# Retention's queries and keys: out of the visited groups, into four wide groups behind them; the gates in their places

## The chip, the cores and the metric

One Trainium2 chip, one of its cores. The metric is the time of one execution on the device in microseconds (us), as the median of several runs. The core's engines are TensorE (PE in the profile, with its weight loads as PEld), VectorE (DVE), ScalarE (ACT), GpSimd (POOL) and SyncE (SP, whose queue issues the loads).

## The reference

One decoder layer for a batch of 1 and 256 tokens, d_model 2048, all in float32, then a final RMSNorm:

```
mod = silu(c) W_ada + b_ada          -> shift1, scale1, gate1, shift2, scale2, gate2
h   = RMSNorm(x)(1+scale1)+shift1
p   = h W_in      # [retention q,k,v,g | HGRN2 q,f,i,g | branch gate A | branch gate B]
yA  = W_retO( LN_head(Retention(rope(q),rope(k),v)) * silu(g) )      # 4 heads of 256
yB  = W_hgO( RMS_head(HGRN2(silu(q), f, i)) * silu(g) )              # 8 heads of 128
x   = x + gate1 * ( (sigmoid(gA)*yA + sigmoid(gB)*yB) W_out )
h2  = RMSNorm(x)(1+scale2)+shift2
[a, b] = split(causal_depthwise_conv3(h2 W_up))                      # d_ff 5632
out = RMSNorm_final( x + gate2 * ((silu(a) * b) W_down) )
```

Retention and HGRN2 run in chunks of 128 tokens. This case is about `p = h W_in`, whose first eight parts are 1024 columns wide each and whose two branch gates are 2048.

## The kernel before

**Numbers and tiles.** Each float32 product is made of three float32r products. Weights and activations are both split into an upper part (the value rounded to float32r) and a lower part (the remainder): upper x upper, upper x lower and lower x upper are added in PSUM. Weights come in pieces of two K tiles (2 x 128 rows) by 512 columns, 512 KB each. `pieces` loads a piece into `raw` (12 buffers), ACT copies it to `wh` (upper part, line 167, 4 buffers) and DVE subtracts to `wl` (lower part, line 172, 4 buffers). An activation tile `hT` has for each K tile 512 columns: 256 tokens of upper parts, then 256 tokens of lower parts. A group is 512 columns of weights over all 16 K tiles.

**Two forms of matmul.** `mm_rows` (lines 196 to 198) makes token rows: the activations (128 tokens) are the stationary operand and 512 weight columns stream; six matmuls of 512 columns a K tile. `mm_cols` (lines 209 to 211) makes channel columns, the transpose: the weights (128 columns) are stationary and 256 tokens stream; twelve matmuls of 256 columns a K tile. The up projection has a third form (lines 1081 and 1083): weights stationary, upper and lower activations side by side stream as one matmul of 512 columns, and the lower weights with the upper activations as one of 256. The two halves of the 512 stand apart in PSUM and are added afterwards.

**PSUM.** `pg` is a tile of two banks with two buffers, `po` one of one bank with four. `mm_rows` and `mm_cols` need one `pg` for a group; the small matmuls of HGRN and retention use `po`.

**Order of the work.** The modulation vectors (`ada1`, DVE dot products of loaded rows, line 421) make the activations one K tile after another, about one in 15 us. So the first twelve groups, `ATT`, are *visited*: the loop goes round them, takes in each as many K tiles as there are by then, and adds the partial product to the group's SBUF tile `p` (`take`: at first an ACT copy, line 789, afterwards a DVE add, line 791). The twelve are HGRN's f, q, i and retention's q, k, v, two groups of 512 columns each; i and v are in rows (`ROWS`), the other eight in columns. When all of a block's three groups are complete, its generator is started: `hgrn` or `retention`, for two halves `hb` of the heads. The last visits, with all 16 K tiles there, go through the groups in order and take from one to five K tiles each.

Behind the loop come four gate groups (`wb`, rows; ACT applies Silu from PSUM to `gt`, line 878), eight branch gate groups (`wab`, rows; Sigmoid, line 892), the output projections of both branches, `wout`, the up projection and the down projection.

The generators in `back[0]` (HGRN, retention, their gating) and `back[1]` (the dot products of gate1 and ada2) are traced in slices by `pump`, which is called once a piece of weights; queue 0 works through one generator after the other. All of it runs on the engines beside the groups' matmuls. `hgrn` uses its gate in its last step (line 682), `gated` that of retention (line 745). Instructions not pinned are ordered by a scheduler at compile time; at run time each engine's queue is in order.

Of the kernel before, what the change touches and what calls it, by code (L numbers as in the profile page):

```python
# [16 lines left out]
AF = mybir.ActivationFunctionType  # L17
ALU = mybir.AluOpType

P = 128  # L20
D = 2048
T = 256
NT = T // P
KT = D // P
# [5 lines left out]
G = 512  # L30
# [8 lines left out]

C_RQ, C_RK, C_RV, C_RG, C_HQ, C_HF, C_HI, C_HG = (i * W1 for i in range(8))  # L40
C_GA, C_GB = 8 * W1, 8 * W1 + D
ATT = (C_HF, C_HF + G, C_HQ, C_HQ + G, C_HI, C_HI + G, C_RQ, C_RQ + G, C_RK, C_RK + G, C_RV, C_RV + G)
ROWS = (C_HI, C_HI + G, C_RV, C_RV + G)
GW = 2 * G
LEVELS = (64, 32, 16, 8, 4, 2, 1)
TWO_PI = 2.0 * math.pi
# [9 lines left out]
class Kernel:  # L56
# [143 lines left out]
    def mm_cols(self, ps, act, wh, wl, first, last):  # L200

        nc = self.nc
        hi, lo = act[:, :T], act[:, T:]
        for j in range(4):
            cs = slice(j * P, (j + 1) * P)

            opens = first and j % 2 == 0
            out = ps[j // 2][:, j % 2 * T : (j % 2 + 1) * T]
            nc.tensor.matmul(out, lhsT=wh[:, cs], rhs=hi, start=opens, stop=False, skip_group_check=True)  # L209
            nc.tensor.matmul(out, lhsT=wh[:, cs], rhs=lo, start=False, stop=False, skip_group_check=True)  # L210
            nc.tensor.matmul(out, lhsT=wl[:, cs], rhs=hi, start=False, stop=last, skip_group_check=True)  # L211

    def products(self, mm, ps, src, act, k0, kts, hold=0, first=True, last=True, gain=None):

# [306 lines left out]
    def hgrn(self, hb, hf, hq, v, gates):  # L521

        nc = self.nc
# [2 lines left out]
        k = self.blk([P, 4, T], name="k")  # L526
        b = self.blk([P, 4, T], name="b")
        nc.scalar.activation(f, hf, AF.Sigmoid)
        yield 3.0
        for h in range(4):  # L530
            g = slice(4 * hb + h, 4 * hb + h + 1)
# [16 lines left out]
        f = None  # L548
        q = self.blk([P, 4, T], name="q")
        nc.scalar.activation(q, hq, AF.Silu)  # L550
        yield 2.0
        at = self.blk([P, 4, T], name="at")
        nc.gpsimd.memset(at, 0.0)
# [9 lines left out]
        ps = self.po()  # L563
# [5 lines left out]
        ps = self.po()  # L569
# [4 lines left out]
        for c in range(2):  # L574
            dst = at[:, :, c * P : (c + 1) * P].rearrange("p h (z x) -> p h z x", x=32)
            msk = self.ident.bitcast(I32).rearrange("p (z x) -> p z x", x=32)[:, None].to_broadcast([P, 4, 4, 32])
            src = ps[:, 4 * c * 32 : 4 * (c + 1) * 32].rearrange("p (h x) -> p h x", h=4)[:, :, None, :].to_broadcast([P, 4, 4, 32])
# [3 lines left out]
        kt = self.blk([P, 4, T], name="kt")  # L581
        nc.gpsimd.memset(kt, 0.0)
        for lev, n in enumerate(LEVELS[:-2]):
# [15 lines left out]
            ps = self.po()  # L599
            for h in range(4):  # L600
                for c in range(2):
                    j = 2 * h + c
# [11 lines left out]
            if n >= 32:  # L614
                for z in range(0, P, 2 * n):
                    for c in range(2):
                        dst = at[z : z + n, :, c * P + z + n : c * P + z + 2 * n]
                        src = ps[z + c * n : z + (c + 1) * n, : 4 * n]
# [28 lines left out]
        ps = self.po()  # L647
        for z in range(2):
            for j in range(4 * z, 4 * z + 4):
                h, c = j // 2, j % 2  # L650
                for x in range(0, P, 32):
# [3 lines left out]
                        lhsT=kt[:, h, c * P + x : c * P + x + 32],  # L655
                        rhs=eq[:, j, :].rearrange("p (l x) -> p l x", l=2)[:, :, x // 2 : x // 2 + 16],
                        start=True,
                        stop=True,
# [3 lines left out]
            self.masked(at, len(LEVELS) - 2 + i, n, ps[:, : 8 * 32].rearrange("p (j l x) -> p j l x", j=8, l=2)[:, :, i, :])  # L662
            yield 0.9
        yield 2.8
        while len(gates) <= hb:
            yield None
        o = self.blk([P, NT, G], name="oh")
        for t in range(NT):
            ps = self.po()
# [85 lines left out]
    def run(self):  # L755
        nc, a = self.nc, self.a
# [23 lines left out]

        accs = [self.blk([P, NT, G] if c0 in ROWS else [P, 4, T], name="p") for c0 in ATT]
        done = [0] * len(ATT)
        mms = [self.mm_rows if c0 in ROWS else self.mm_cols for c0 in ATT]

        def take(g, ps, fresh):
            for at, z in self.parts(ps, ATT[g] in ROWS):
                dst = accs[g][:, at, :]
                if fresh:
                    nc.scalar.activation(dst, z, AF.Copy)  # L789
                else:  # L790
                    nc.vector.tensor_tensor(dst, dst, z, ALU.add)
# [7 lines left out]
        ps = [self.po2(), self.po2(), self.pg(), self.pg()][:FIRST]  # L799
        for k in range(2):  # L800
# [12 lines left out]
            for g in range(FIRST):  # L813
                if g >= ahead:
                    rests.append(self.rest(uppers[g] if g < len(uppers) else self.upper(a["wa"][g][:, k : k + 1, :], 1, G)))
                wh, wl = rests[g]
# [14 lines left out]

        work = 2 * FIRST
        g = FIRST
        att, gates = [], []
        small = False
        while min(done) < KT:
            if work > SMALL and not small:
                small = True
                self.small_loads(nc.sync, ("freq", "lbT", "lmask"))
                self.start(self.trig())  # L840
                self.start(self.lower_bound())
            have = min(KT, 2 + int((work - LAG) / ADA_EVERY))
            m = have - done[g]
            if m > 0:
                self.finish(*ada[:have])
                if g < RESIDENT:
                    self.products(mms[g], ps[g], a["wa"][g], act, done[g], m, first=False, last=have == KT)
                    if have == KT:
                        take(g, ps[g], True)
                else:  # L850
                    take(g, self.products(mms[g], self.pg(), a["wa"][g], act, done[g], m), done[g] == 0)
                done[g] = have
                work += m
                for hb in range(2):
                    for kind, first in ((self.hgrn, 0), (self.retention, 6)):
                        gs = [first + hb, first + 2 + hb, first + 4 + hb]
                        if g in gs and min(done[i] for i in gs) == KT:
                            self.pace(0, 14.0, 24)
                            att.append(self.start(kind(hb, *(accs[i] for i in gs), gates)))
            else:  # L860
                work += 0.5
            g = (g + 1) % len(ATT)
            if have == KT and done[0] < KT:
                g = min(i for i in range(len(ATT)) if done[i] < KT)
        self.xT = None
        del accs
        self.small_loads(nc.sync, ("gn2", "convw"))

# [2 lines left out]
        self.pace(0, 143.0, 88)  # L871
        self.pace(1, 68.0, 96)
        sgb, sga = [], []
        for j in range(4):
            ps = self.rows(a["wb"][j], act)
            gt = self.blk([P, NT, G], name="gt")
            for at, z in ps:
                nc.scalar.activation(gt[:, at, :], z, AF.Silu)
            gates.append(gt)

        og = [[], []]

# [6 lines left out]
        for j in range(8):  # L889
            gt = self.blk([P, NT, G], name="gt")  # L890
# [40 lines left out]
        for j in range(4):  # L931
            last = j == 3
            x1.append(self.load_rows(j))
            if not last:
                g = self.row(self.gate["gate1"], j, "g1")
            if j == 2:
                g3 = self.row(self.gate["gate1"], 3, "g1")
            elif last:
                g = g3
            ps = self.products(self.mm_rows, self.po2() if last else self.pg(), a["wout"][j], actm, 0, KT, hold=4 * last, gain=g if last else None)  # L940
            if last:
                g = None
# [229 lines left out]
def _groups(w, starts):  # L1172
    return np.stack([_pack(w[:, s : s + G]) for s in starts])
# [23 lines left out]
def _arrays(x, c, positions, w_ada, b_ada, g_norm1, w_in, w_ret_o, w_hg_o, w_out, hg_lb, g_norm2, w_up, conv_w, conv_b, w_down, g_final):  # L1197
    cols = lambda v: np.ascontiguousarray(v.reshape(-1, P).T)
    wada, win, wup = w_ada[0], w_in[0], w_up[0]
    out = {  # L1200
        "xT": _pack(np.ascontiguousarray(x[0].T)),
        "c": c.reshape(1, D),
        "pos": positions.reshape(1, T),
        "gn1": cols(g_norm1[0]),
        "gn2": cols(g_norm2[0]),
        "lbT": np.ascontiguousarray(hg_lb.reshape(2, HH, P).transpose(2, 0, 1)),
        "convw": np.ascontiguousarray(np.concatenate([conv_w[0], conv_b], axis=0).reshape(4, 2 * FT, P).transpose(2, 0, 1)),
        "gf": g_final.reshape(1, D),
        "xR": np.ascontiguousarray(x[0].reshape(NT, P, D).transpose(1, 0, 2)),
        "wb": _groups(win, [C_HG, C_HG + G, C_RG, C_RG + G]),  # L1210
        "wab": _groups(win, [z + j * G for z in (C_GB, C_GA) for j in range(4)]),
        "whg": _groups(w_hg_o[0], [j * G for j in range(4)]),
        "wret": _groups(w_ret_o[0], [j * G for j in range(4)]),
        "wout": _groups(w_out[0], [j * G for j in range(4)]),
        "wdown": _groups(w_down[0], [j * G for j in range(4)]),
        "wup": np.stack([_pack(np.concatenate([wup[:, 2 * i * P : 2 * (i + 1) * P], wup[:, FF + 2 * i * P : FF + 2 * (i + 1) * P]], axis=1)) for i in range(FT // 2)]),
    }
    out["wa"] = _groups(win, ATT)
    adaT = np.concatenate([wada.T, b_ada[0][:, None]], axis=1).reshape(6, KT, P, D + 1)
    out["ada1"] = np.ascontiguousarray(adaT[[1, 0]].transpose(1, 0, 2, 3))  # L1220
    out["ada2"] = np.ascontiguousarray(adaT[[4, 3]].transpose(1, 0, 2, 3))
    out["gate1"] = adaT[2]
    out["gate2"] = adaT[5]
    out.update(_tables())
    return out
# [22 lines left out]
```

## Time and profile before

| | |
|---|---|
| median of 3 runs | 1516.57 us (1516.51 to 1517.36) |
| profiled execution: span | 1514.7 us |
| PE, PEld busy | 1498.0 us (99%), 1288.4 us (85%) |
| DVE, ACT busy | 1205.9 us (80%), 845.4 us (56%) |
| loads | 382.11 MB read from HBM, 254 GB/s over the span |
| visited loop | from the first visit to about 295 us |
| gate groups `wb` | 294.9 to 394.0 us |
| branch gate groups `wab` | 394.0 to 592 us |
| up projection, down projection | about 772 to 1267 us, 1267 to 1507 us |

The profile is of one execution, whose span is 1.9 us shorter than the median of the runs; what lies outside the span (start and end of the program) is in the median and not in the span. Times in the timeline are from the start of the span. A matmul's duration there is its way through the array, and the next one starts before it ends. `[1.64 <-PE pg L211]` at the end of a row is the idle time of that engine ahead of the instruction, and what ended it. `x2` merges two instructions that follow on each other.

### The profile page before, as it was taken

What the parts mean: (1) busy time and instruction counts of PE and PEld (TensorE: products, weight loads), DVE (VectorE), ACT (ScalarE), POOL (GpSimd) and SP (SyncE); (2) the same over time, 40 slices, a digit from 0 to 9 for tenths busy, and PEclk for the clock granted to TensorE, in tenths of its full rate; (3) what the DMA queues carried; (4) which work ended last, traced back from release to release, by engine and by line L of the source; (5) the groups of instructions that cost most, each with busy time, mean ns of one, the idle gap of its engine ahead of it and who ended that gap; (6) DMA issues with size and microseconds to landing.
All of it is one profiled execution on the core that took longest, in us unless ns stands there. A gap on an engine that the chain in (4) does not pass through costs nothing.

```text
span 1514.7 us, 23095 instructions
## 1 busy us (share of the span) xinstructions
PE 1498.0 (99%) x8722; PEld 1288.4 (85%) x8722; DVE 1205.9 (80%) x1639; ACT 845.4 (56%) x1207; POOL 4.0 (0%) x8
## 2 busy tenths in 40 slices
PE   8999999999999999999999999999999999999997
PEld 6999999878788888888888888888888888888886
DVE  7899996898999877898977778778777769455694
ACT  6645454768775644445466555555555558344343
POOL 0000000000000000000000000000000000000000
PEclk9999999999999999999999999999999999999999
DMA  9999997777888889989847777777777666667651
GB/s 376 377 344 332 316 325 228 229 275 266 287 264 289 275 288 329 320 289 358 310 133 242 237 230 233 228 233 231 230 245 228 220 187 196 201 209 215 177 178 56
DMA packets 110997, 385.75 MB, mean 255 GB/s; under 512 B 12803, under 2 KB 13347, under 8 KB 110885
## 3 DMA queue, kind: packets, MB, share of 16 engines
q1 hardware_dynamic: 110016, 383.14, 76.7%
q8 instruction: 68, 1.11, 0.3%
q10 hardware_dynamic: 868, 1.13, 0.2%
q14 instruction: 45, 0.36, 0.1%
HBM read 382.11 MB, written 2.11 MB: 254 GB/s over the span
## 4 chain that ended last, share of the span: by engine, by line
PE 95%; ACT 2%; DVE 1%; DMA 1%; issue 0%; SPq 0%; DVEq 0%; ACTq 0%
PE pg L196 13%; PE pg L197 13%; PE pg L198 13%; PE po L1081 11%; PE pg L1081 10%; PE po L1083 5%; PE pg L1083 5%; PE po L197 3%; PE po L198 3%; PE po L196 3%; PE pg L209 3%; PE pg L211 3%; PE pg L210 3%; PE po L209 1%; PE po L210 1%; PE po L211 1%
## 5 line engine op out<-in xcount | busy, mean ns | idle before, releaser
L167 ACT ACTIVATE wh<-raw 128x1024 fp32r<-128x1024 f32 (+1 forms) x536 | 550.6, 1033 | 523.2 <-PE pg L198 183.4
L172 DVE TENSOR_TENSOR wl<-raw,wh 128x1024 fp32r<-128x1024 f32 (+1 forms) x536 | 634.5, 1190 | 248.2 <-ACT wh L167 247.4
L421 DVE SCALAR_TENSOR_TENSOR raw<-raw,sc 128x1024 f32<-128x1024 f32 x192 | 233.5, 1219 | 0.0
L1081 PE MATMUL po<-h2T,wh 128*128 128x512 f32 x704 | 221.1, 395 | 0.0
L1081 PE MATMUL pg<-h2T,wh 128*128 128x512 f32 x688 | 216.4, 396 | 0.0
L196 PE MATMUL pg<-wh,hT 128*128 128x512 f32 x512 | 203.1, 397 | 0.2 <-ACT p L789 0.2
L197 PE MATMUL pg<-wl,hT 128*128 128x512 f32 x512 | 200.5, 392 | 1.7 <-DVE wl L172 1.7
L198 PE MATMUL pg<-wh,hT 128*128 128x512 f32 x512 | 199.6, 390 | 0.0
L1083 PEld LDWEIGHTS po<-h2T,wl 128*128 128x128 f32 x704 | 132.2, 188 | 31.3
L1083 PEld LDWEIGHTS pg<-h2T,wl 128*128 128x128 f32 x688 | 129.1, 188 | 31.0 <-DVE wl L172 0.5
L1083 PE MATMUL po<-h2T,wl 128*128 128x256 f32 x704 | 138.3, 278 | 0.0
L1083 PE MATMUL pg<-h2T,wl 128*128 128x256 f32 x688 | 135.3, 278 | 0.1
L197 PEld LDWEIGHTS pg<-wl,hT 128*128 128x128 f32 x512 | 96.2, 188 | 22.1 <-DVE wl L172 3.3
L198 PEld LDWEIGHTS pg<-wh,hT 128*128 128x128 f32 x512 | 96.1, 188 | 20.2
L196 PEld LDWEIGHTS pg<-wh,hT 128*128 128x128 f32 x512 | 96.2, 188 | 19.9 <-ACT p L789 0.4
L211 PE MATMUL pg<-hT,wl 128*128 128x256 f32 x384 | 109.0, 284 | 0.6 <-DVE wl L172 0.6
L209 PE MATMUL pg<-hT,wh 128*128 128x256 f32 x384 | 109.2, 284 | 0.1
L210 PE MATMUL pg<-hT,wh 128*128 128x256 f32 x384 | 109.0, 284 | 0.0
L1081 PEld LDWEIGHTS po<-h2T,wh 128*128 128x128 f32 x704 | 107.1, 189 | 0.0
L1081 PEld LDWEIGHTS pg<-h2T,wh 128*128 128x128 f32 x688 | 104.7, 189 | 0.0
L211 PEld LDWEIGHTS pg<-hT,wl 128*128 128x128 f32 x384 | 74.0, 193 | 0.8 <-DVE wl L172 0.8
L209 PEld LDWEIGHTS pg<-hT,wh 128*128 128x128 f32 x384 | 74.1, 193 | 0.6 <-ACT wh L167 0.2
(250 smaller groups left out, 2208.3 us busy)
## 6 DMA issues: line engine op xcount, KB each, us to landing
raw<-in_wup SPq DMA_DIRECT2D x176, 512.0 KB, 4.5
raw<-in_wdown SPq DMA_DIRECT2D x88, 512.0 KB, 4.3
raw<-in_wa SPq DMA_DIRECT2D x80, 512.0 KB, 6.0
raw<-in_ada SPq DMA_DIRECT2D x64, 512.5 KB, 5.7
raw<-in_ada SPq DMA_DIRECT2D x64, 512.0 KB, 5.8
raw<-in_wab SPq DMA_DIRECT2D x64, 512.0 KB, 5.1
raw<-in_gate SPq DMA_DIRECT2D x32, 512.5 KB, 4.8
raw<-in_wb SPq DMA_DIRECT2D x32, 512.0 KB, 5.0
```

Of the source, the lines that this page charges most:

```text
L167: self.pin(self.nc.scalar.activation(wh, raw, AF.Copy))
L172: self.last = self.nc.vector.tensor_tensor(wl, raw, wh.bitcast(F32), ALU.subtract)
L196: nc.tensor.matmul(ps[t], lhsT=hi, rhs=wh, start=first, stop=False)
L197: nc.tensor.matmul(ps[t], lhsT=hi, rhs=wl, start=False, stop=False)
L198: nc.tensor.matmul(ps[t], lhsT=lo, rhs=wh, start=False, stop=last)
L209: nc.tensor.matmul(out, lhsT=wh[:, cs], rhs=hi, start=opens, stop=False, skip_group_check=True)
L210: nc.tensor.matmul(out, lhsT=wh[:, cs], rhs=lo, start=False, stop=False, skip_group_check=True)
L211: nc.tensor.matmul(out, lhsT=wl[:, cs], rhs=hi, start=False, stop=last, skip_group_check=True)
L421: dot = self.pin(nc.vector.scalar_tensor_tensor(raw[:, 0, :], raw[:, 0, :], 1.0, self.sc[:, u * GW : u * GW + w], ALU.mult, ALU.mult, accu ...
L1081: self.pin(nc.tensor.matmul(ps[j + z], lhsT=wh[:, cs[z]], rhs=act, start=kt == 0, stop=False, skip_group_check=bool(begun)))
L1083: nc.tensor.matmul(ps[j + z][:, :T], lhsT=wl[:, cs[z]], rhs=act[:, :T], start=False, stop=kt == KT - 1, skip_group_check=bool(begun))
```

## The change

The four groups of retention's queries and keys leave `ATT`, and the four gate groups (HGRN's and retention's) take their places, in rows. A gate group that is complete gets its Silu in place, in SBUF. Behind the loop, where the gate groups were, the four query and key groups are made by `wide_group`: weights stationary, upper and lower activations streaming side by side, in the form of the up projection; each group takes both buffers of `pg`, and in each piece of two K tiles the first two column blocks (pair 0) are done for both K tiles and then the other two (pair 2). At the end ACT copies the half of the lower activations of a pair to SBUF and DVE adds the other half from PSUM. `retention` is started there, for each half of the heads when its query and its key group are made. Some tiles are given up earlier in the trace (`hf`, `hq`, `accs[i]`). `gates` is now a dictionary.

```diff
-ATT = (C_HF, C_HF + G, C_HQ, C_HQ + G, C_HI, C_HI + G, C_RQ, C_RQ + G, C_RK, C_RK + G, C_RV, C_RV + G)
-ROWS = (C_HI, C_HI + G, C_RV, C_RV + G)
+GATES = (C_HG, C_HG + G, C_RG, C_RG + G)
+ATT = (C_HF, C_HF + G, C_HQ, C_HQ + G, C_HI, C_HI + G, *GATES, C_RV, C_RV + G)
+ROWS = (C_HI, C_HI + G, *GATES, C_RV, C_RV + G)
+KEYS = (C_RQ, C_RK, C_RQ + G, C_RK + G)
...
+    def mm_wide(self, ps, act, wh, wl, first, last, pair):
+
+        nc = self.nc
+        cs = [slice(z * P, (z + 1) * P) for z in (pair, pair + 1)]
+        for z in range(2):
+            nc.tensor.matmul(ps[pair + z], lhsT=wh[:, cs[z]], rhs=act, start=first, stop=False)
+        for z in range(2):
+            nc.tensor.matmul(ps[pair + z][:, :T], lhsT=wl[:, cs[z]], rhs=act[:, :T], start=False, stop=last)
+
+    def wide_group(self, src, act):
+
+        nc = self.nc
+        pgs = [self.pg(), self.pg()]
+        ps = pgs[0][:2] + pgs[1][:2]
+        for step in self.pieces(src, KT):
+            for pair in (0, 2):
+                for kt, wh, wl in step:
+                    self.mm_wide(ps, act(kt), wh, wl, kt == 0, kt == KT - 1, pair)
+            self.pump(len(step) / 2)
+        out = self.blk([P, 4, T], name="p")
+        for pair in (0, 2):
+            dst = out[:, pair : pair + 2, :]
+            z = pgs[pair // 2][2]
+            nc.scalar.activation(dst, z[:, :, T:], AF.Copy)
+            nc.vector.tensor_tensor(dst, dst, z[:, :, :T], ALU.add)
+        return out
...
-        while len(gates) <= hb:
+        while hb not in gates:
             yield None
...
-        att, gates = [], []
+        att, gates = [], {}
+
+        def begin(kind, hb, *ins):
+            att.append(self.start(kind(hb, *ins, gates)))
...
+                if have == KT and ATT[g] in GATES:
+                    nc.scalar.activation(accs[g], accs[g], AF.Silu)
+                    gates[GATES.index(ATT[g])] = accs[g]
                 for hb in range(2):
-                    for kind, first in ((self.hgrn, 0), (self.retention, 6)):
-                        gs = [first + hb, first + 2 + hb, first + 4 + hb]
-                        if g in gs and min(done[i] for i in gs) == KT:
-                            self.pace(0, 14.0, 24)
-                            att.append(self.start(kind(hb, *(accs[i] for i in gs), gates)))
+                    gs = [hb, 2 + hb, 4 + hb]
+                    if g in gs and min(done[i] for i in gs) == KT:
+                        self.pace(0, 14.0, 24)
+                        begin(self.hgrn, hb, *(accs[i] for i in gs))
+                        for i in gs:
+                            accs[i] = None
...
+        v = accs[10:]
         del accs
...
-        for j in range(4):
-            ps = self.rows(a["wb"][j], act)
-            gt = self.blk([P, NT, G], name="gt")
-            for at, z in ps:
-                nc.scalar.activation(gt[:, at, :], z, AF.Silu)
-            gates.append(gt)
+        for hb in range(2):
+            begin(self.retention, hb, *[self.wide_group(a["wk"][2 * hb + i], act) for i in range(2)], v.pop(0))
...
-        "wb": _groups(win, [C_HG, C_HG + G, C_RG, C_RG + G]),
+        "wk": _groups(win, KEYS),
```

More of the change, by code (lines that the diff above doesn't have):

```diff
@@ L528, in hgrn @@
         nc.scalar.activation(f, hf, AF.Sigmoid)
+        hf = None
         yield 3.0
@@ L550, in hgrn @@
         nc.scalar.activation(q, hq, AF.Silu)
+        hq = None
         yield 2.0
```

## The prediction

> **What bounds the kernel now.** First the page: its engines, and the chain that ended last.
>
> ```profile
> span 1514.7 us, 23095 instructions
> ...
> PE 1498.0 (99%) x8722; PEld 1288.4 (85%) x8722; DVE 1205.9 (80%) x1639; ACT 845.4 (56%) x1207; POOL 4.0 (0%) x8
> ...
> PE 95%; ACT 2%; DVE 1%; DMA 1%; issue 0%; SPq 0%; DVEq 0%; ACTq 0%
> ```
>
> TensorE (PE) carries 95% of the chain. Its busy time overlaps neighbouring matmuls, so a price is the step from one start to the next, never a duration. Then the stretches that the change touches: the visited loop (to about 295 us), its tail, and the four gate groups behind it (295 to 394 us).
>
> ```profile
> core 0: us, PE busy (x) PEld busy (x) DVE busy (x) ACT busy (x) POOL busy (x), PEclk, DMA share, GB/s
> 225.51:232.71 7.20, 7.20 (x62) 7.19 (x60) 6.11 (x10) 3.43 (x5) 0.00 (x0) 1.00 0.99 346
> 220.07:225.51 5.44, 5.44 (x25) 4.51 (x24) 5.44 (x7) 2.86 (x5) 0.00 (x0) 1.00 0.99 328
> ...
> 40.00:260.00 220.00, 220.00 (x1584) 208.77 (x1583) 195.44 (x255) 118.12 (x168) 1.91 (x2) 1.00 0.93 322
> 260.00:300.00 40.00, 39.45 (x235) 34.89 (x235) 32.41 (x40) 30.64 (x36) 0.00 (x0) 1.00 0.69 224
> 300.00:400.00 100.00, 98.81 (x790) 79.97 (x789) 89.24 (x124) 76.65 (x111) 1.91 (x2) 1.00 0.80 276
> ```
>
> The clock is full (1.00). From 40 to 260 us PE has no idle. Behind that it has little, while VectorE (DVE) is 89% and ScalarE (ACT) 77% busy: an instruction that PE must wait for can stand in a queue there. DMA is nearly full in the visited loop (0.93).
>
> Third, the step of each kind of matmul, from the timeline of PE: rows (L196 on), columns (L209 on) and, from the up projection, the form that the change takes over (L1081, L1083).
>
> ```profile
> 222.12 0.39 PE L196 MATMUL pg<-wh,hT 128*128 128x512 f32 x1
> 222.34 0.39 PE L197 MATMUL pg<-wl,hT 128*128 128x512 f32 x1
> ...
> 225.51 0.28 PE L209 MATMUL pg<-hT,wh 128*128 128x256 f32 x1
> 225.63 0.28 PE L210 MATMUL pg<-hT,wh 128*128 128x256 f32 x1
> ...
> 1000.59 0.63 PE L1081 MATMUL pg<-h2T,wh 128*128 128x512 f32 x2
> 1001.05 0.39 PE L1083 MATMUL pg<-h2T,wl 128*128 128x256 f32 x2
> 1001.28 0.62 PE L1081 MATMUL pg<-h2T,wh 128*128 128x512 f32 x2
> ```
>
> The stretch 220.07:225.51 is one visit of four K tiles in rows: 5.44/24 = 0.2267 us a matmul, 1.36 us a K tile of six. 225.51:232.71 is five K tiles in columns: 7.20/60 = 0.120 us, 1.44 us a K tile of twelve. Two wide pairs go from 1000.59 to 1001.28, 0.695 us, so 1.39 us a K tile of eight matmuls. All three stream the same 3072 columns; they differ in what each matmul costs beyond its columns.
>
> **The change, part by part.**
>
> *PE.* Four groups of 16 K tiles go from columns to wide; gates stay in rows and only move. 64 x (1.39 - 1.44) = -3.2 us. Two starts of the chain view that lie six K tiles apart give the wide one more closely:
>
> ```profile
> 1000.75 0.47 PE pg L1081 x2
> ...
> 1009.11 0.47 PE pg L1081 x2
> ```
>
> 8.36/6 = 1.393 us, and 64 x (1.393 - 1.44) = -3.0 us, which I take. By place: the visited loop gets 64 x (1.36 - 1.44) = -5.1 us, the groups behind it 64 x (1.393 - 1.36) = +2.1 us.
> The Trainium skill (TensorE: Matmul & The Clock Gate, Back-to-back issue gap) puts a warm matmul at N/2.4 + 2.5 ns: 109 ns for 256 columns and 216 ns for 512, by which this term would be an estimated 64 x (1300 - 1310) ns = -0.6 us, and the sum 2.4 us higher. The trace has 120 and 227 ns, so a matmul here costs more beyond its columns than the page says; the trace decides.
>
> *Does the visited loop give the 5.1 us?* It does if activations keep ahead. The last one against its first use:
>
> ```profile
> 241.91 0.42 DVE L350 TENSOR_TENSOR hT<-h,hT 128x256 fp32r<-128x256 f32 x1
> ...
> 251.43 0.28 PE L209 MATMUL pg<-hT,wh 128*128 128x256 f32 x1
> ```
>
> It is ready at 242.3 and used at 251.4 us, 9 us ahead; even if loads and dots did not move at all, 5 us less leaves 4. The bytes and issues of the loads are the same. I take all of it; the other end, nothing, is a rival.
>
> *PSUM, the new wait.* A row group holds one `pg` of two, so the next group starts in the other. A wide group holds both. Its last two K tiles do pair 0 first (8 matmuls, 1.39 us) and then pair 2, so pair 0 has 1.39 us to be read out: an ACT copy and a DVE add, each 128x512, one after the other. Nearest rows for their durations, and for the time that such a read-out waits in its queue:
>
> ```profile
> L1030 DVE TENSOR_TENSOR gp<-pg,g 128x512 f32<-128x512 f32 x10 | 6.4, 683 | 0.4 <-PE pg L198 0.4
> ```
>
> ```profile
> 315.14 0.58 ACT L567 ACTIVATE a<-po 128x512 f32<-128x512 f32 x1
> ...
> 245.55 0.28 PE L211 MATMUL pg<-hT,wl 128*128 128x256 f32 x1
> ...
> 245.87 1.22 DVE L791 TENSOR_TENSOR p<-p,pg 128x1024 f32<-128x1024 f32 x1 [1.64 <-PE pg L211]
> ...
> 294.65 0.39 PE L198 MATMUL pg<-wh,hT 128*128 128x512 f32 x1
> 296.01 1.22 DVE L791 TENSOR_TENSOR p<-p,pg 128x1024 f32<-128x1024 f32 x1
> ...
> 318.65 1.03 ACT L878 ACTIVATE gt<-pg 128x1024 f32<-128x1024 f32 x1 [1.11 <-PE pg L198]
> ...
> 343.93 0.39 PE L198 MATMUL pg<-wh,hT 128*128 128x512 f32 x1
> 345.20 1.03 ACT L878 ACTIVATE gt<-pg 128x1024 f32<-128x1024 f32 x1
> ...
> 370.24 0.39 PE L198 MATMUL pg<-wh,hT 128*128 128x512 f32 x1
> 370.46 0.39 PE L196 MATMUL pg<-wh,hT 128*128 128x512 f32 x1
> 371.61 0.18 DVE L274 RECIPROCAL rsh<-rsh 128x4 f32<-128x4 f32 x1 [3.99 <-ACT rsh L273]
> 372.89 1.03 ACT L878 ACTIVATE gt<-pg 128x1024 f32<-128x1024 f32 x1
> ```
>
> From a group's last matmul (start plus duration) to its read-out it took 0.04 us (245.83 to 245.87), 0.97 (295.04 to 296.01), 0.88 (344.32) and 2.26 (370.63). Today this costs PE nothing: at 370.46 the next group runs while the read-out waits. Pair 0's result lands some 0.16 us (0.28 less one step of 0.12) after its last step, so the floor of the stall at a change of groups is -1.39 + 0.16 + 0.04 + 0.58 + 0.04 + 0.68 + 0.1 for the way back (an estimate) = 0.2 us. With queue waits of 0.4 us on ACT and 0.5 on DVE (half an instruction at 77 and 89% busy) it is 1.1 us. The upper end, with 2.26 on one queue, is 2.5 us; the DVE idle of 3.99 us behind one reciprocal shows that a queue can stand longer. Four such changes (wide to wide three times, wide to branch gate once): 0.8 to 10 us, taken as 4.4. Ahead of the first wide group only pair 2 waits, for the last visit's add: 0.16 + 0.04 to 0.97 + 1.22 + 0.1 - 1.39 = 0.1 to 1.1 us, taken as 0.6. Together +5.0.
> The Trainium skill (Perfetto Trace Analysis, Matmuls) asks that independent groups rotate through PSUM banks so that the read-out of one overlaps the next group's matmuls; the row 370.46 agrees, and this change gives that up for four groups.
>
> *The tail of the visited loop.* Four gates get their Silu in place, 1.03 us each as at L878, three of them, by the loop's order, behind visits of one K tile near 276 to 282 us.
>
> ```profile
> 278.11 2.73 ACT L167 ACTIVATE wh<-raw 128x1024 fp32r<-128x1024 f32 x3
> 281.94 1.06 ACT L167 ACTIVATE wh<-raw 128x1024 fp32r<-128x1024 f32 x1 [1.11 <-PE pg L210]
> 285.56 1.07 ACT L167 ACTIVATE wh<-raw 128x1024 fp32r<-128x1024 f32 x1 [2.56 <-DVE wl L172]
> ...
> 282.73 0.50 PE L197 MATMUL pg<-wl,hT 128*128 128x512 f32 x1 [0.48 <-DVE wl L172]
> ...
> 376.66 0.50 PE L197 MATMUL pg<-wl,hT 128*128 128x512 f32 x1 [0.38 <-DVE wl L172]
> ```
>
> ```profile
> 385.93 0.50 PE pg L197
> ```
>
> ACT has 1.11 + 2.56 = 3.7 us to spare there, against 3 x 1.03 = 3.1; but weights come late already (282.73). 0 to 3 us, taken as +1. On the other side four Silus with their table loads leave the stretch 318 to 396 us, where PE waits for late weights at 376.66 and, in the chain, ahead of 385.93 us; their going is worth 0 to 1.7 us (0.6 + 1.1 beyond the step), taken as -1.
>
> *What else moves.* Eight adds and eight copies of 128x512 are new: 5.5 us of DVE and 4.6 of ACT over 90 us, hidden behind PE but for the read-outs above; that they slow weights is in the tail's upper end. Retention now starts behind the wide groups, but takes its turn behind both HGRN blocks in the same queue:
>
> ```profile
> L691 DVE TENSOR_TENSOR rtmp<-p,sin x4: 1192/1216/1221, 453.8 to 492.3; 128x1024 f32<-128x1024 f32 x4
> ```
>
> It starts at 453.8 us, nearly 60 us after the last wide group can be done (the gate groups ended at 394): nothing. The SP queue issues as many loads of equal size: nothing. HGRN waited for no gate: the first was there at 319.7 us (318.65 + 1.03), well ahead of HGRN's last step: nothing.
>
> *Sum.* -3.0 + 5.0 + 1 - 1 = +2.0 us on the profiled span, 1516.7; the median of the runs is 1.9 us above that span (1516.57 - 1514.7), so 1518.6, say 1518.5 us. I call 0.2% (3.0 us) about what a measurement tells from no change: 1513.5 to 1519.6 is the same.
>
> **The rivals.**
> 1. *The read-outs stand in queues* (slower). At three or four of the changes of groups the copy or the add stands behind an HGRN instruction that waits itself, as at 371.61. At 2.2 us a change: -3.0 + 9.4 + 1 = +7.4, 1524 us. It decides from 1.6 us a change on. For it: 89% busy DVE, 2.26 us at 370.63. Against it: 0.04 us at 245.83, and read-outs come early in the order. Chance 0.33.
> 2. *The read-outs stay at their floor* (faster). 4 x 0.2 + 0.1 = 0.9 us of stalls, and the weights at 376 and 385 us in time: -3.0 + 0.9 - 1.7 = -3.8, 1512.8 us. Against it: both engines would have to be free at each change. Chance 0.12.
> 3. *The visited loop does not get shorter*, since its loads, at 0.93 of the DMA engines, set its pace. Then +2.1 + 5.0 = +7.1, 1523.7 us. Against it: no wait of PE between 40 and 260 us, 9 us ahead at the last activation. Chance 0.07.
>
> **How the numbers follow.** Forecast 0.48: 1518.5 us, no change that can be told. Rivals 1 and 3 give slower, 0.40; rival 2 faster, 0.12. The forecast's own range is 1515 to 1520. The range asked for goes from rival 2's 1513 to the upper ends of the stalls (-3.0 + 11 + 3 - 1 = +10): 1513 to 1526.
>
> **What would show it.** Each of L209 to L211 falls from 512 to 256 matmuls on `pg` and `po`, the new pair has 256 each at 0.348 us a pair. The loop's last visit ends some 5 us sooner. At four places, some 25 us apart from about 315 us on, PE stands 0.2 to 2.5 us on a `pg` read-out by DVE; row groups show none. Wrong would be stalls that are nowhere or over 3 us each, a visited loop of the old length, or PE waiting on weights behind the Silus.

## The result, and the profile after

The changed kernel takes 1520.86 us (median of 7 runs, 1520.47 to 1521.77), the kernel before 1516.7 us beside it: a ratio of 1.0029, 95% interval 1.002 to 1.0038. It is slower by 4.2 us. Its profiled execution has a span of 1519.9 us, 5.2 us more than that of before.

The page of the changed kernel, engines and chain:

```profile
span 1519.9 us, 22606 instructions
...
PE 1497.0 (98%) x8466; PEld 1276.6 (84%) x8466; DVE 1211.8 (80%) x1647; ACT 843.7 (56%) x1210; POOL 4.0 (0%) x8
...
PE 91%; DVE 5%; ACT 2%; DMA 1%; issue 1%; SPq 0%; DVEq 0%; ACTq 0%
```

There are 256 matmuls fewer, and DVE has come into the chain: 5%, from 1%. Where PE waited for DVE stands in the view of waits, between 294 and 402 us (total, times, longest):

```profile
PE pg L220 <- DVE p L239: 3.3, 2, 2.7
...
PE pg L198 <- DVE p L239: 1.2, 1, 1.2
```

L220 is the first matmul of a wide group, L198 that of the branch gates, and L239 the add that reads a wide group out. The timeline of PE shows three of the four changes of groups, and in the middle one ACT and DVE stand below:

```profile
319.30 0.72 PE L220 MATMUL pg<-hT,wh 128*128 128x512 f32 x2 [0.61 <-DVE p L239]
...
373.81 0.73 PE L220 MATMUL pg<-hT,wh 128*128 128x512 f32 x2 [2.70 <-DVE p L239]
...
399.13 0.50 PE L198 MATMUL pg<-wh,hT 128*128 128x512 f32 x1 [1.19 <-DVE p L239]
```

```profile
370.19 1.28 ACT L302 ACT_TABLE_LOAD   x1
371.49 0.30 ACT L302 ACTIVATE rsh<-ssh,eps 128x4 f32<-128x4 f32 x1
371.69 1.06 ACT L238 ACTIVATE p<-pg 128x512 f32<-128x512 f32 x2
...
371.82 0.18 DVE L303 RECIPROCAL rsh<-rsh 128x4 f32<-128x4 f32 x1 [3.99 <-ACT rsh L302]
372.03 1.13 DVE L713 SCALAR_TENSOR_TENSOR oh<-po,rsh,p 128x128 f32<-128x128 f32 x4
373.07 1.27 DVE L239 TENSOR_TENSOR p<-p,pg 128x512 f32<-128x512 f32 x2
```

At 371 us the read-out stands in both queues behind the end of HGRN's first half: the ACT copy behind the square root (371.49) and the table load of 1.28 us that comes with it, the DVE add behind the reciprocal, which waited 3.99 us for that root, and four multiplications. ACT is the larger part. Pair 0's result is there at about 369.72 us (its last matmul's start plus duration); its copy starts at 371.69, 1.97 us later, and ends at 372.27 us; its add starts at 373.07, another 0.80 us later, and takes 0.68 us. PE goes on at 373.81. Then comes a thing that no part of the sum had. The view by windows:

```profile
core 0: us, PE busy (x) PEld busy (x) DVE busy (x) ACT busy (x) POOL busy (x), PEclk, DMA share, GB/s
...
372.00:374.00 2.00, 0.20 (x1) 0.20 (x2) 1.97 (x6) 2.00 (x4) 0.00 (x0) 1.00 0.08 33
374.00:375.00 1.00, 1.00 (x6) 0.87 (x6) 1.00 (x2) 1.00 (x2) 0.00 (x0) 1.00 0.00 0
375.00:378.50 3.50, 3.50 (x14) 2.97 (x13) 3.38 (x5) 2.83 (x4) 0.00 (x0) 0.51 0.50 143
378.50:382.00 3.50, 3.50 (x22) 3.06 (x21) 1.99 (x6) 3.47 (x4) 0.00 (x0) 1.00 0.96 258
```

PEclk falls to half for 3.4 us about 1.3 us after PE has gone on: 14 matmuls in 3.5 us where the next 3.5 us hold 22. That costs 1.7 us. The four changes of groups cost 0.8, 0.3, 2.9 and 1.3 us beyond the matmuls' own steps, 5.3 together.

In the visited loop the steps are as priced. Sixteen K tiles of four changed groups ran from 154.84 to 177.87 us before and run from 155.21 to 176.97 us now, 23.03 and 21.76 us, that is 0.08 us less a K tile. But the loop ends only 1 us sooner, at 293.83 instead of 294.88. Three new stalls and a later start took most of the rest:

```profile
70.56 0.39 PE L213 MATMUL po<-hT,wl 128*128 128x256 f32 x1 [0.16 <-DVE wl L174]
...
120.20 0.50 PE L199 MATMUL pg<-wl,hT 128*128 128x512 f32 x1 [1.03 <-DVE wl L174]
...
284.41 0.50 PE L199 MATMUL pg<-wl,hT 128*128 128x512 f32 x1 [1.13 <-DVE wl L174]
```

All three are lower weights that come late. The last stands behind the gates' Silus, on ACT:

```profile
276.72 1.28 ACT L890 ACT_TABLE_LOAD   x1
278.01 2.14 ACT L890 ACTIVATE p<-p 128x1024 f32<-128x1024 f32 x2
280.06 1.04 ACT L169 ACTIVATE wh<-raw 128x1024 fp32r<-128x1024 f32 x1
281.36 1.06 ACT L890 ACTIVATE p<-p 128x1024 f32<-128x1024 f32 x1 [0.26 <-DVE p L822]
282.32 2.51 ACT L169 ACTIVATE wh<-raw 128x512 fp32r<-128x512 f32 x3
```

The account of the span: loop steps -5.1, stalls of the loop +1.7 (at 70 and 119 us, 0.3 and 1.2, and the slower steps right beside them) and +1.4 (tail), start of the run +0.7; groups' steps +2.1, read-outs +5.3, half clock +1.7, weights late before at 376 and 385 us and not now -1.5. That makes +6.3 for a measured +5.2; some 1 us less is lost around HGRN's small matmuls, and this was not followed further. The 0.7 us at the start is chance: up to 33 us both programs are the same, and a second profile of the changed kernel (span 1518.9 us) does not have it.

### The profile page after: what moved, and what is told of

It is laid out like the page before. It is cut to its first block, busy times and chain, and to the rows that moved or that the text cites. A ratio compares the mean times of both kernels' runs of the same rounds, so it can differ in the third digit from the quotient of the medians.

```text
span 1519.9 us, 22606 instructions
## 1 busy us (share of the span) xinstructions
PE 1497.0 (98%) x8466; PEld 1276.6 (84%) x8466; DVE 1211.8 (80%) x1647; ACT 843.7 (56%) x1210; POOL 4.0 (0%) x8
## 4 chain that ended last, share of the span: by engine, by line
PE 91%; DVE 5%; ACT 2%; DMA 1%; issue 1%; SPq 0%; DVEq 0%; ACTq 0%
PE pg L198 13%; PE pg L199 13%; PE pg L200 13%; PE po L1117 11%; PE pg L1117 10%; PE po L1119 5%; PE pg L1119 5%; PE po L200 3%; PE po L199 3%; PE po L198 3%; PE pg L220 3%; DVE wl L174 2%; PE pg L222 1%; DVE raw L450 1%; PE po L213 1%
## 5 line engine op out<-in xcount | busy, mean ns | idle before, releaser
L450 DVE SCALAR_TENSOR_TENSOR raw<-raw,sc 128x1024 f32<-128x1024 f32 x192 | 233.7, 1219 | 0.0
L198 PE MATMUL pg<-wh,hT 128*128 128x512 f32 x512 | 202.2, 395 | 1.3 <-DVE p L239 1.2
L198 PEld LDWEIGHTS pg<-wh,hT 128*128 128x128 f32 x512 | 96.1, 188 | 21.8 <-DVE p L239 1.4
L220 PE MATMUL pg<-hT,wh 128*128 128x512 f32 x256 | 82.3, 404 | 3.4 <-DVE p L239 3.3
L200 PE MATMUL pg<-wh,gs 128*128 128x512 f32 x176 | 68.6, 390 | 0.0
L199 PE MATMUL pg<-wl,gs 128*128 128x512 f32 x176 | 68.5, 389 | 0.0
L198 PE MATMUL pg<-wh,gs 128*128 128x512 f32 x176 | 68.5, 389 | 0.0
L198 PE MATMUL po<-wh,gs 128*128 128x512 f32 x176 | 68.5, 389 | 0.0
```

Source lines behind the costliest of these rows:

```text
L198: nc.tensor.matmul(ps[t], lhsT=hi, rhs=wh, start=first, stop=False)
L199: nc.tensor.matmul(ps[t], lhsT=hi, rhs=wl, start=False, stop=False)
L200: nc.tensor.matmul(ps[t], lhsT=lo, rhs=wh, start=False, stop=last)
L220: nc.tensor.matmul(ps[pair + z], lhsT=wh[:, cs[z]], rhs=act, start=first, stop=False)
L450: dot = self.pin(nc.vector.scalar_tensor_tensor(raw[:, 0, :], raw[:, 0, :], 1.0, self.sc[:, u * GW : u * GW + w], ALU.mult, ALU.mult, accu ...
```

## The experiments

Theory A: the read-outs of both `pg` buffers stand on PE's path. Theory B: the exchange itself costs (the loop, retention's later start). Theory C: the wide matmuls are slower than in the up projection. The runs are compared with 1517.1 us for the kernel before, beside them.

**More time for the read-out.** The last four K tiles go pair by pair.

```diff
+        held = []
         for step in self.pieces(src, KT):
+            held += step
+            if step[-1][0] == KT - 3:
+                self.pump(len(step) / 2)
+                continue
             for pair in (0, 2):
-                for kt, wh, wl in step:
+                for kt, wh, wl in held:
                     self.mm_wide(ps, act(kt), wh, wl, kt == 0, kt == KT - 1, pair)
+            held = []
```

> The changed kernel, but a wide group's last four K tiles are done pair by pair (pair 0 for all four, then pair 2), so pair 0 has 2.79 us instead of 1.39 to be read out. Theory A (the read-outs of both pg buffers stand on TensorE's path): the stalls of 0.8, 0.3 and 1.35 us at three changes of groups go, the one of 2.9 us shrinks to about 1.5 and the half clock behind it goes or shrinks: 1515 to 1517.5 us. Theory B (the exchange costs, that is the visited loop or retention's later start, not the read-outs): no change, 1520.9 us within 1. Theory C (the wide matmuls themselves are slower than in the up projection): no change either, and a step other than 0.348 us a pair.

1515.97 us (ratio 0.9991, 0.9982 to 1.0). PE has no stall at any change of groups, and the clock stays full. By windows, at the place of the long stall:

```profile
370.00:374.00 4.00, 4.00 (x25) 3.40 (x24) 2.98 (x7) 3.99 (x8) 0.00 (x0) 1.00 0.12 46
375.00:378.50 3.50, 3.50 (x22) 3.06 (x21) 3.42 (x4) 3.47 (x4) 0.00 (x0) 1.00 0.85 222
```

It gained more there than the 1.4 us of lead: pair 0's copy now came ahead of the table load in ACT's queue (367.83 and 368.88 us) and its add ahead of the reciprocal in DVE's (368.45 and 370.50 us), so neither stood behind HGRN.

**Another place in PSUM.** Pair 2 goes to two `po`, so the next group starts in the other `pg`.

```diff
-        pgs = [self.pg(), self.pg()]
-        ps = pgs[0][:2] + pgs[1][:2]
+        z0 = self.pg()
+        ps = z0[:2] + self.po2()[:2]
...
```

The read-out of pair 2 is then two copies and two adds of half the size.

> The changed kernel, but pair 0 of a wide group stands in one pg and pair 2 in two po, so the next group can begin in the other pg while this one is read out. Theory A: all four stalls (5.3 us) and the half clock (1.7 us) go: about 1514 us, 1513 to 1516; up to 2 us of it lost if HGRN's small matmuls have to wait for the two po that are left. Theory B: 1520.9 us or more. Theory C: 1520.9 us.

1514.95 us (0.9984, 0.9975 to 0.9993). This is the sharpest test, since the queues stand as they did: the reciprocal still waits 3.84 us on DVE, and PE now runs through it at full clock.

```profile
371.28 0.18 DVE L303 RECIPROCAL rsh<-rsh 128x4 f32<-128x4 f32 x1 [3.84 <-ACT rsh L302]
```

```profile
370.00:374.00 4.00, 4.00 (x25) 3.47 (x24) 2.68 (x9) 3.99 (x8) 0.00 (x0) 1.00 0.57 226
375.00:378.50 3.50, 3.50 (x22) 3.05 (x21) 3.38 (x6) 3.50 (x4) 0.00 (x0) 1.00 0.65 171
```

So 5.9 of the changed kernel's 1520.86 us were the read-outs and the half clock that the longest of them brought; priced from its trace they were 7.0. In the traces the four groups take 98.7 us (105.3 in the changed kernel, 99.1 before).

**Columns instead of wide.** `wide_group` is replaced by `mm_cols` in one `pg`, with one ACT copy; the gates stay in the loop.

> The changed kernel, but the four query and key groups behind the loop are made by columns in one pg each, read out by one ACT copy; the gates stay in the visited loop. Theory A: steps cost 64 x (1.44 - 1.393) = +3.0 us, the stalls at changes of groups (5.3 us) and the half clock (1.7 us) go: 1520.9 + 3.0 - 7.0 = about 1517 us. Theory B: 1520.9 + 3.0 = about 1524 us. Theory C: below 1517 by what the wide matmuls are slower.

1517.63 us (1.0005, 0.9996 to 1.0014). Theory A's 1517; B and C fall. Against the run with two `po`, which also has no read-out stalls, it is 2.7 us slower: that is the worth of the wide form with its own read-out, 3.0 by the steps. Against the kernel before it says that the exchange alone changes nothing: what the loop's steps gain, the groups behind it lose, and stalls move from one place to the other.

**Silus later.** Each gate's Silu is traced behind a wide group.

```diff
-                    nc.scalar.activation(accs[g], accs[g], AF.Silu)
-                    gates[GATES.index(ATT[g])] = accs[g]
+                    raws[GATES.index(ATT[g])] = accs[g]
...
+                made.append(self.wide_group(a["wk"][2 * hb + i], act))
+                z = raws.pop(2 * hb + i)
+                nc.scalar.activation(z, z, AF.Silu)
...
```

> The changed kernel, but each gate's Silu is traced behind one of the wide groups instead of at the end of its last visit. Theory A with the Silus as the cause of late weights at 279 to 283 us: the stalls there fall from 2.4 us to the 1.0 us of before, so 1519.5 us, if the Silus and their table loads do no harm among the wide groups (up to +1.5 if they do). If the late weights there have another cause: the stalls stay, 1520.9 us or more.

1520.54 us (1.002, 1.001 to 1.0029). In its trace the stall near 283 us is gone and those near 278 to 280 us, which the kernel before had, stay; but a new one of 0.5 us comes at 294 us, where PE waits for the last visit's add (L822), and the long one with its half clock is as before. 0.3 us of difference to the changed kernel can't be told from none. With the read-outs out of the way it shows:

> The run with pair 2 in two po (1514.95 us) and the run with the Silus behind the wide groups put together. Theory: with the read-outs off the path the late Silus cost nothing among the wide groups, and the visited loop keeps the 1.3 us of its tail: 1513.7 us, 1513 to 1515. If the Silus among the groups give back what the tail gains, as the stall of 0.51 us at 294 us in the run with late Silus suggests: 1515.

1513.17 us (0.9973, 0.9962 to 0.9984), 1.8 us below the run with two `po` alone, where 1.3 was expected.

**The loop's other stalls.** Near 70 us the order differs on ACT, while DVE waits 2.1 us for it. The read-out of a row visit is still an ACT copy there. Before, the weights stand ahead of it:

```profile
66.36 1.05 ACT L167 ACTIVATE wh<-raw 128x1024 fp32r<-128x1024 f32 x1
67.42 1.03 ACT L789 ACTIVATE p<-pg 128x1024 f32<-128x1024 f32 x1
```

In the changed kernel they stand behind it, and behind a scale:

```profile
67.09 1.03 ACT L820 ACTIVATE p<-pg 128x1024 f32<-128x1024 f32 x1 [2.87 <-PE pg L200]
...
68.19 1.05 ACT L169 ACTIVATE wh<-raw 128x1024 fp32r<-128x1024 f32 x1
...
69.27 1.23 DVE L174 TENSOR_TENSOR wl<-raw,wh 128x1024 fp32r<-128x1024 f32 x1 [2.10 <-ACT wh L169]
```

Near 119 us DVE is busy throughout, and the weights come late in its queue. Two read-outs of row visits (L822) stand in other places there than before. The first goes ahead of a dot product (L450) that ACT's next scale waits for; before, the same dot product started at 111.42 and the read-out stood behind it, at 112.95 us. The second goes ahead of an activation, a dot product and the lower weights (118.92) that PE waits for until 120.20 us:

```profile
112.29 1.22 DVE L822 TENSOR_TENSOR p<-p,pg 128x1024 f32<-128x1024 f32 x1
113.43 1.22 DVE L450 SCALAR_TENSOR_TENSOR raw<-raw,sc 128x1025 f32<-128x1025 f32 x1
...
116.31 1.21 DVE L822 TENSOR_TENSOR p<-p,pg 128x1024 f32<-128x1024 f32 x1
117.45 0.41 DVE L379 TENSOR_TENSOR hT<-h,hT 128x256 fp32r<-128x256 f32 x1
117.78 1.21 DVE L450 SCALAR_TENSOR_TENSOR raw<-raw,sc 128x1024 f32<-128x1024 f32 x1
...
118.92 1.22 DVE L174 TENSOR_TENSOR wl<-raw,wh 128x1024 fp32r<-128x1024 f32 x1
```

First another pace of the dot products (`self.pace(1, 4.6, ADA_EVERY / 2)` for 4):

> The same, and the dot products of the visited loop are traced 15% earlier (rate 4.6 for 4). Theory: the stall of 1.2 us near 119 us and that of 0.3 us near 70 us come from the order of ACT's and DVE's queues, where a read-out of a row visit stands ahead of a dot product and the scale that waits for it; another pace gives another order, and the two stalls go: 1.0 to 1.5 us less than the run without it. Rival: rows leave DVE too little time in the loop, so weights are late whatever the order: the stalls stay or move, the time is the same within 0.5 us.

1514.1 us (0.9981, 0.9972 to 0.999). The theory's gain did not come: the stall of 0.3 us near 70 us stayed, that of 1.2 us near 119 us shrank to 0.5, and another of 0.6 came at 141 us. A pace moves the dots and cannot say which order is the good one. Then the order itself: a visit's read-out is traced one visit later, but for the first and the last visits.

```diff
...
-                    take(g, self.products(mms[g], self.pg(), a["wa"][g], act, done[g], m), done[g] == 0)
+                    made = self.products(mms[g], self.pg(), a["wa"][g], act, done[g], m)
+                    if held:
+                        take(*held.pop())
+                    if have < KT and work > 20:
+                        held.append((g, made, done[g] == 0))
+                    else:
+                        take(g, made, done[g] == 0)
...
```

> The run with two po and late Silus (1513.2 us), but in the visited loop a visit's read-out into its SBUF tile is traced one visit later, so that dot products and weights stand ahead of it in DVE's queue more often. Theory (the loop's stalls at 70 and 119 us come from read-outs of row visits that stand ahead of a dot product or of weights): the stall of 1.2 us at 119 us shrinks or goes, 1512 to 1513 us. Rival (DVE has too little time in the loop, whatever the order): a stall of the same size stays or shows up elsewhere, 1513.2 us or more.

1512.57 us (0.9968, 0.9956 to 0.9981). Both stalls are gone; the stretch 116 to 122 us, in the run with two `po` and late Silus and then in this one:

```profile
116.00:122.00 6.00, 4.97 (x23) 3.89 (x22) 6.00 (x10) 2.52 (x4) 0.96 (x1) 1.00 0.91 331
```

```profile
116.00:122.00 6.00, 6.00 (x33) 5.03 (x32) 6.00 (x10) 1.48 (x4) 0.08 (x1) 1.00 0.95 309
```

DVE is as full as before (6.00 of 6.00) and PE loses nothing there. In this run's DVE queue the second read-out stands behind the weights:

```profile
116.75 1.22 DVE L174 TENSOR_TENSOR wl<-raw,wh 128x1024 fp32r<-128x1024 f32 x1
117.89 1.21 DVE L822 TENSOR_TENSOR p<-p,pg 128x1024 f32<-128x1024 f32 x1
```

The first one is still ahead of its dot product (111.25 and 112.38 us), so the second was the one that made the stall. Near 70 us ACT's weights (67.14) now stand ahead of the copy (69.60). It was the order, not too little time, though not all is won: two shorter stalls, of 0.24 and 0.21 us, come at 124.2 and 127.4 us. The 0.6 us between the medians alone would not show it, since their intervals overlap; the trace does.

> The run with two po and late Silus, but the gate groups of the visited loop are made by columns, not rows (their values then stand in the wrong places of the gate tiles; every other step, the Silus and the sizes are as they were). In the loop this is what stood there before the change. Theory (row visits in the gates' places bring the loop's stalls at 70 and 119 us): both are gone, and the loop is 64 x 0.08 = 5.1 us longer less 1.5 us: about 1516.8 us. Rival (the stalls come from something else, such as the loads): they stay, 1518.3 us.

1516.25 us (0.9995, 0.9986 to 1.0004). With columns in the gates' places both stalls are gone too, and up to 286 us the order on DVE is that of before. So it is the row visits that bring the other order. Against the run with rows there it is 3.1 us slower, where 3.6 was expected.

**The changed kernel once more**, for its profile:

> The changed kernel again, for its profile. The stalls at 70, 119, 279 to 283, 318, 371 and 398 us come back with the same lengths, and the half clock of 3.4 us near 375 us too, if both are of the program. The idle time and the half clock near 25 us, where the program is the same as before, differ from run to run.

1520.69 us, one run. All the stalls named come back within 0.05 us, and so does the half clock's length, though it begins 0.2 us before PE goes on (372.68 and 372.87 us) and not 1.3 us after; the clock near 25 us was full this time, where the first profile had a drop. The half clock here:

```profile
372.50:376.00 3.50, 3.13 (x9) 2.67 (x10) 3.38 (x5) 3.50 (x4) 0.00 (x0) 0.53 0.20 26
```

## Why the prediction was right or wrong

The measured 1520.86 us lies in the range, but not in the forecast: 1518.5 us with "no change that can be told" was the likeliest, and the kernel is slower by more than its 0.2%. It ended on the side of rival 1, but not by rival 1's mechanism: the changes of groups cost 1.3 us each on average, below the 1.6 us from which that rival was to decide. That the time lies in the range says little, since the range was 13 us wide. One of the prediction's own signs of being wrong came, PE waiting on weights behind the Silus (284.41), and another nearly did: the loop ended 1 us sooner instead of 5.

- *PE, -3.0 us*: right. The loop's steps give 0.08 us a K tile as priced, and wide against columns with no read-out stalls in either is 2.7 us. The Trainium skill (TensorE: Matmul & The Clock Gate, Back-to-back issue gap) gives the formula that the prediction sets beside this term for a matmul in isolation, and not for a stream with weight loads as here.
- *PSUM, +5.0 us*: right in place and size, 5.3 us. Its spread was told rightly too (0.3 to 2.9 us a change, for 0.2 to 2.5), and the row that was quoted as a warning, the reciprocal that waits 3.99 us, stands in the longest. The prediction's own sum gives that one when the measured waits are put in: -1.39 + 0.16 + 1.97 on ACT + 0.58 + 0.80 on DVE + 0.68 + 0.06 for the way back (373.75 to 373.81, taken as 0.1 without a row) = 2.86 us. So most of it was ACT's queue, with the table load, and not the reciprocal. Wrong was the 0.6 us ahead of the first wide group: PE went from 293.61 to 293.83 without a stall. In the run with late Silus that wait did come, at 0.5 us.
- *The clock*: missing. The sum priced the idle of PE and not what PE does after it. The 2.7 us of idle brought 3.4 us at half clock, 1.7 us. The Trainium skill (TensorE: Matmul & The Clock Gate, Part 1: The HAM clock gate) has half and full clock as the two states and a window of 3413 ns, and the trace agrees with both (0.51 in the result's row 375.00:378.50, for 3.4 us); it puts the drop behind at least one idle window of about 3.4 us, and here 2.7 us was enough.
- *"Does the visited loop give the 5.1 us? I take all of it"*: this is the step that failed most. It asked whether activations and loads keep ahead, and they do. It did not ask what a row visit in place of a column visit does to the order of DVE's and ACT's queues: read-outs went ahead of the weights that PE needed next, on ACT at 70 us and on DVE at 119 us, and that cost 1.7 us. Rival 3 had the loop not get shorter, but for the loads' sake; nothing in the runs shows that.
- *Tail, +1*: right in mechanism, measured +1.4. *Weights at 376 and 385 us, -1*: they are gone, -1.5.
- *Adds, retention's start, loads, gates: nothing*: the time behind the wide groups, from the first branch gate matmul to PE's last, is 1112.7 us in both kernels.

So the terms that were there sum to about what they measured; what made the forecast short are the two that were not: order in the loop (1.7 us) and clock (1.7 us). Both follow from a stall or a queue rather than from an instruction's cost. The later start (+0.7) and the smaller losses around HGRN's matmuls (-1), for which the sum had no terms, nearly cancel, and that is luck.

## What to carry to other kernels

Before an accumulation group takes all of PSUM's buffers, follow its read-out through each in-order queue and look for an instruction there that waits itself; if there is one, place half of the group in banks of another pool, which here turned 4.2 us lost into 2.2 us won (1514.95 against 1517.1). When a form of matmul is exchanged in a scheduled loop, compare the order of the other engines' queues as well as the steps of PE: the cheaper form can put a read-out ahead of the work that feeds the next matmuls. The best version here, wide groups over two pools, late Silus and later read-outs in the loop, takes 1512.57 us, ratio 0.9968 (0.9956 to 0.9981) to the kernel before.

## What the runs showed of the hardware

A single idle of PE of 2.7 us, behind a loop that had been at full clock, was followed by 3.4 us at half clock, in all three profiled runs that had that idle (both of the changed kernel and the one with late Silus), and in none of the others at that place. At the start, where PE also waits, 1.5 us of idle and 0.4 us shortly after brought the same drop in two profiles (the first of the changed kernel, and columns instead of wide), and 0.6 to 1.3 us and 0.4 did not in the others. The window of 24 to 28 us of the changed kernel, first profile and second:

```profile
24.00:28.00 4.00, 2.45 (x14) 2.04 (x14) 3.59 (x8) 2.43 (x6) 0.00 (x0) 0.87 1.03 410
```

```profile
24.00:28.00 4.00, 2.88 (x22) 2.47 (x21) 3.62 (x8) 2.48 (x6) 0.00 (x0) 1.00 1.03 410
```

The drop keeps no fixed distance from the end of the idle: it came 1.3 us after it in the first profile of the changed kernel, 0.2 us before it in the second, and 0.2 us after it with late Silus (373.51 and 373.26 us). It keeps to a grid instead. In the first profile the clock changes at 26.93, 30.34, 375.09 and 378.50 us, and these times lie 1, 101 and 1 times 3.413 us apart. Cut along this grid, the stretch just ahead of the long stall's drop, and the one of half clock behind it, are:

```profile
371.67:375.09 3.42, 1.28 (x7) 1.11 (x8) 3.24 (x8) 3.42 (x6) 0.00 (x0) 1.00 0.11 46
```

```profile
375.09:378.50 3.41, 3.41 (x13) 2.92 (x12) 3.29 (x5) 2.74 (x4) 0.00 (x0) 0.50 0.52 147
```

So 2.1 us of idle in one stretch brought it. At the start, the run with columns instead of wide had 1.5 us of idle in its stretch, and the clock dropped; the run with more time for the read-out had 1.4 us, and it did not. First the one, then the other:

```profile
24.28:27.69 3.41, 1.91 (x14) 1.50 (x13) 3.03 (x7) 2.82 (x6) 0.00 (x0) 1.00 1.03 410
```

```profile
24.29:27.70 3.41, 2.03 (x15) 1.62 (x14) 3.02 (x7) 2.56 (x6) 0.00 (x0) 1.00 1.04 413
```

In these eleven profiles the border lies near 1.5 us of idle in one stretch of 3.413 us; one stretch with 1.5 us at the end of the second profile (1509.32 to 1512.73) did not drop, so it is not told more closely. By these figures, as an estimate, an idle of 2.7 us that the grid cuts into halves of 1.35 would bring no drop; no run here had one.
